# Moving a small transposition, four scalings and the first loads in a two-layer float32 trunk on one Trainium2 core

## The chip, the cores and the metric

The kernel runs on one core of one Trainium2 chip. The metric is device time in microseconds (us): the median of three runs of the kernel before is 1584.31 us (1582.89 to 1584.82).

## The reference, cut to what matters

Two layers over x (256 tokens x 2048 columns), 16 heads of 128. Each layer normalizes x, scales and shifts it by a modulation of the condition c, runs attention, gates it with silu(z), projects it and adds it to x, multiplied by the modulation's third part, the gate.

```python
cond = jax.nn.silu(c)
for i in range(2):
    mod = cond @ mod_w[i] + mod_b[i]
    shift, scale, gate = jnp.split(mod[:, None, :], 3, axis=-1)
    h = rms_norm(x, norm_w[i]) * (1.0 + scale) + shift
    y = mixer(h, w_in[i]) @ w_out[i]   # layer 0: 3 dilated groups, w_in 2048 x 20480
    x = x + gate * y                   # layer 1: block attention, w_in 2048 x 8192
return rms_norm(x, final_norm_w)
```

## The kernel before, in words

Every weight matrix is read once, in units of two halves (128 rows x 512 columns each, 512 KB a unit). A unit's raw float32 lands in a ring of five buffers; ScalarE rounds it to a high part `wh` (L347) and VectorE subtracts to get the low part `wl` (L353). TensorE multiplies in three products: high by high, high by low, low by high. So VectorE and ScalarE convert while TensorE multiplies, and a ring of four converted units limits how far ahead they can be (`plan_conversions`).

The order is written out by hand. A list of steps is built first; the last loop then emits, for each step `i`: its matmuls, the tasks hung on it with `at_once` (evacuations of PSUM), the low parts of the units whose conversion was emitted one step earlier (`finish_converts`), the new conversions, and the tasks hung on it with `at`. Every engine runs its own instructions in that order. A task at step `i` therefore stands, on each engine's queue, behind all that was emitted up to it.

The modulation of layer 0 and 1 is not a matmul. `mod_unit` loads 512 KB of mod_w and VectorE multiplies it by the broadcast condition and sums it (L143, two instructions of 512 columns); four such units make one 128-wide row of shift and scale.

The places that the change touches:

- **Start.** SyncE loads the small weights, both halves of x (`xin`, 128 tokens each), four mod units, then weights. `start_rstd` (L199) sums squares, on VectorE for the first half of x and on ScalarE for the second. GpSimd scales x (L234), TensorE transposes it.
- **First 256 steps.** Each is one half unit by one 128-row chunk k of the normalized input ("row k"). Row k exists only after four of its mod units: `rows_ready(k)` (L248) adds them up and writes `hA` high (L256) and low (L262). `READY` (L579) says at which step each row may be used first; the mod units of row k are hung on the steps before, and `rows_ready(k)` on `READY[k] - 3`. A planner (L584) then lays out visits: it takes the output part that is least far along and multiplies all rows that are ready. The first visit of a part ends in a copy on ScalarE (L565), each later one in two additions on VectorE (L567).
- **Gate.** Mod units of the third part are spread over later steps by `add_pieces` (L171). At the step after the last one `gate_write` (L155) sums them on VectorE (L149), transposes the 128 x 16 result on TensorE into `pgt` (L161), copies it and writes it to DRAM; `gate_read` broadcasts it back. This happens once per layer. The gate is used in the output projection, hundreds of steps later in both layers.
- **Border.** Between the layers `norm_transpose` (L723) transposes x with the scale on the diagonal (L728) and applies scale and shift to four blocks of 128 columns, n of them on VectorE (L736) and the others on ScalarE (L738); `norm_split` makes the high part on ScalarE (L194) and the low part on VectorE (L195). Step `mid` ends the first half of the tokens, `last` the second.

Of the kernel before, what the change touches and what calls it, by code (L numbers as in the profile page):

```python
# [12 lines left out]
F32 = mybir.dt.float32  # L13
F32R = mybir.dt.float32r
AF = mybir.ActivationFunctionType
ALU = mybir.AluOpType
AX = mybir.AxisListType

P = 128
S = 256  # L20
D = 2048
# [3 lines left out]
EPS = 1e-6  # L25
# [28 lines left out]
def trunk_kernel(ctx: ExitStack, tc: tile.TileContext, x, c, small_w, mod_t, weights, final_norm_w, dmask, out, laid_out):  # L54


    nc = tc.nc
    pool = lambda name, bufs, **k: ctx.enter_context(tc.tile_pool(name=name, bufs=bufs, **k))
    const = pool("const", 1)
# [6 lines left out]
    tmpp = pool("tmpp", 1)  # L66
    small = pool("small", 4)
    actp = pool("actp", 1)
# [9 lines left out]
    x_v = x[0].rearrange("(m a) d -> m a d", a=2)  # L78
# [5 lines left out]
    xin = [ypool.tile([P, D], F32, name=f"xin{i}", tag=f"y{2 + i}") for i in range(2)]  # L84
# [1 line left out]
    for i in range(2):  # L86
        nc.scalar.dma_start(c_row[i][0:1], c[:, i * 1024:(i + 1) * 1024])
    smalls = const.tile([P, 128], F32, name="smalls")
    nc.sync.dma_start(smalls, small_w)
    nwT, mbT = smalls[:, 0:2 * KC], smalls[:, 2 * KC:]  # L90
    gate = [const.tile([P, 1024], F32, name=f"gate{i}") for i in range(2)]
    dm = const.tile([P, 9 * P], F32, name="dm")
# [4 lines left out]
    nhalf = const.tile([P, 2], F32, name="nhalf")  # L97
    nc.gpsimd.memset(nhalf, -0.5)
    cb = [const.tile([P, 512], F32, name=f"cb{i}") for i in range(4)]
    eps = const.tile([P, 1], F32, name="eps")  # L100
    nc.gpsimd.memset(eps, EPS)
    modq = const.tile([P, 96, 4], F32, name="modq")
    modc = const.tile([P, 96], F32, name="modc")
    sc0 = const.tile([P, KC], F32, name="sc0")
# [30 lines left out]
    def mod_unit(layer, b, half):  # L135

        early = layer == 0 and b < 32 and b % 16 > 0
        raw = next(early_raw) if early else rawp.tile([P, 1024], F32, name="raw", tag="raw")
        nc.sync.dma_start(raw, mod_t[layer, b, half])
        m = 48 * layer + b  # L140
        for i in range(2):
            part, q = raw[:, i * 512:(i + 1) * 512], 2 * half + i
            nc.vector.tensor_tensor_reduce(part, part, cb[q], 1.0, 0.0 if q else mbT[:, m:m + 1],  # L143
                                           ALU.mult, ALU.add, modq[:, m, q:q + 1])

    def mod_sums(m, n, step=1):

        cols = slice(m, m + (n - 1) * step + 1, step)
        nc.vector.tensor_reduce(modc[:, cols], modq[:, cols], axis=AX.X, op=ALU.add)  # L149
# [5 lines left out]

    def gate_write(layer):

        mod_sums(48 * layer + 32, 16)
        scratch[layer] = dram.tile([KC, P], F32, name=f"gate_rows{layer}", tag=f"g{layer}")
        pt = ps_y.tile([P, 512], F32, name="pgt", tag="y")  # L160
        nc.tensor.transpose(pt[:KC, :P], modc[:, 48 * layer + 32:48 * layer + 48], ident)  # L161
        rows = small.tile([P, P], F32, name="grows", bufs=1)
        nc.scalar.activation(rows[:KC], pt[:KC, :P], AF.Copy)
        nc.gpsimd.dma_start(scratch[layer], rows[:KC])
# [6 lines left out]
    def add_pieces(i0, i1, layer, part):  # L171

        for n in range(32):
            at(i0 + n * (i1 - i0) // 32, mod_unit, layer, 16 * part + n // 2, n % 2)
        if part == 2:
            at(i1 + 1, gate_write, layer)
            at(i1 + 3, gate_read, layer)

    def scale_b():
        mod_sums(48, 32)  # L180
# [3 lines left out]
    def rstd_of(ss, n):  # L184

        r = small.tile([P, 2], F32, name="rstd")
        nc.vector.tensor_scalar(r[:, :n], ss, 1.0 / D, EPS, op0=ALU.mult, op1=ALU.add)
        nc.gpsimd.tensor_tensor(r[:, :n], r[:, :n], nhalf[:, :n], op=ALU.pow)
        return r

    def split(dst, src):

        hi = dst[:, :, 0]
        nc.scalar.activation(hi, src, AF.Copy)  # L194
        nc.vector.tensor_tensor(dst[:, :, 1], src, hi.bitcast(F32), op=ALU.subtract)  # L195
# [3 lines left out]
    def start_rstd(tt):  # L199
        ss = small.tile([P, 2], F32, name="ss0")  # L200
        sq = tmpp.tile([P, 1024], F32, name="sq", tag="tmp")
        st = small.tile([P, 1], F32, name="ss1")
        if tt == 0:
            for i in range(2):
                xi = xin[tt][:, i * 1024:(i + 1) * 1024]
                nc.vector.tensor_tensor_reduce(sq, xi, xi, 1.0, 0.0, ALU.mult, ALU.add, ss[:, i:i + 1])
            nc.vector.tensor_tensor(st, ss[:, 0:1], ss[:, 1:2], op=ALU.add)
            start_r.append(rstd_of(st, 1))
            return
        for i in range(2):  # L210
            nc.scalar.activation(sq, xin[tt][:, i * 1024:(i + 1) * 1024], AF.Square, accum_out=ss[:, i:i + 1])
            nc.scalar.activation(st, ss[:, i:i + 1], AF.Identity, scale=1.0 / D, bias=st if i else eps)
        r = small.tile([P, 2], F32, name="rstd")
        nc.gpsimd.tensor_tensor(r[:, 0:1], st, nhalf[:, 0:1], op=ALU.pow)
        start_r.append(r)

    def start_first(tt):

        xc = xin[tt][:, 0:P]
        nc.scalar.activation(xc, xc, AF.Copy, scale=start_r[tt][:, 0:1])  # L220
        if tt == 0:
            slots["first"] = ps_s.tile([P, 512], F32, name="pxt", tag="s")
        pt = slots["first"]
        nc.tensor.transpose(pt[:, tt * P:(tt + 1) * P], xc, ident)
        if tt == 1:
            nc.scalar.activation(xnT[0][:, 0], pt[:, 0:S], AF.Copy)
# [101 lines left out]
    def at(i, f, *a):  # L328
        tasks.setdefault(i, []).append((f, a))
# [21 lines left out]
    def finish_converts(c=slice(0, 2)):  # L351
        for raw, wh, wl in to_finish:
            nc.vector.tensor_tensor(wl[:, c], raw[:, c], wh[:, c].bitcast(F32), op=ALU.subtract)  # L353
        if c.stop == 2:
            to_finish.clear()
# [166 lines left out]
    def product(p, key, st, n, u, first, last):  # L522
        def pe():
            moving(group_ps(key), st, (2 * u, 2 * u + 1), conv[n], (0, 1), first, last)
        return add_step(n, pe)
# [51 lines left out]

    first_parts = [(0, p) for p in PARTS] + [(1, p) for p in PARTS[:EARLY]]
    READY = [0]  # L579
    for n in (9, 9, 10, 11, 11) + (12,) * 10:  # L580
        READY.append(READY[-1] + n)
    done = [0] * len(first_parts)
    visits, t = [], 0
    while min(done) < KC:  # L584
        n_ready = sum(r <= t for r in READY)
        n = done.index(min(done)) if n_ready < KC else next(i for i, d in enumerate(done) if d < KC)
# [18 lines left out]
    for k in range(1, KC):  # L605
        i0, i1 = READY[k - 1], READY[k]
# [8 lines left out]
    for j in range(1, 4):  # L615
# [4 lines left out]
        for n, p in enumerate(PARTS[EARLY:] if j == 1 else PARTS):  # L620
# [3 lines left out]
            for u in range(8):  # L624
                m = add_unit(wA, u, COL[p] * D + j * GC)
                i = product(p, ("A", j, p), st_a, m, u, u == 0, u == 7)
# [79 lines left out]
    b0, mid, last = out_steps("A", "a_w_out", epilogue("A"), True)  # L706
# [7 lines left out]
    hB_box = []  # L714
# [8 lines left out]
    def norm_transpose(tt, g):  # L723
        if not hB_box:
            hB_box.append(hpool.tile([P, KC, 2, S], F32R, name="hB", tag="h"))
        pt = (ps_s, ps_o, ps_t, ps_y)[g].tile([P, 512], F32, name="pxt", tag="soty"[g])
        for b in range(4):
            nc.tensor.matmul(pt[:, b * P:(b + 1) * P], X[g][:, tt, b * P:(b + 1) * P], rB[tt], start=True, stop=True)  # L728
        hf = tp.tile([P, 4, P], F32, name="t")
        hs = tmpp.tile([P, 2, P], F32, name="hs", tag="tmp")  # L730
        n = 3 - g % 2
        for b in range(4):
            k = 4 * g + b
            src, a, s = pt[:, b * P:(b + 1) * P], abB[:, k:k + 1], modc[:, 48 + k:49 + k]
            if b < n:
                nc.vector.tensor_scalar(hf[:, b], src, a, s, op0=ALU.mult, op1=ALU.add)  # L736
            else:
                nc.scalar.activation(hs[:, b - n], src, AF.Identity, scale=a, bias=s)  # L738
        hfB[tt, g] = (n, hf[:, :n], hs[:, :4 - n])

    def norm_split(tt, g):
        n, hf, hs = hfB[tt, g]
        split(hB_box[0][:, 4 * g:4 * g + n, :, tt * P:(tt + 1) * P], hf)
        split(hB_box[0][:, 4 * g + n:4 * g + 4, :, tt * P:(tt + 1) * P], hs)

    for tt, i in enumerate((mid, last)):
        at_once(i, norm_b, tt)
        for g, n in enumerate((3, 5, 9, 11) if tt == 0 else (4, 5, 6, 8)):
            at_once(i + n, norm_transpose, tt, g)
            at(i + n, norm_split, tt, g)  # L750
# [3 lines left out]
    for j in range(4):  # L754
# [4 lines left out]
        for p in PARTS_B:  # L759
            col = COL_B[p] * D + j * GC  # L760
            if j == 0 and p == "v":
                ns = [add_unit(wB, u, col, HOLD[u] if u < 4 else None)
                      for u in range(8)]
                for tt in range(2):
                    for u, n in enumerate(ns):
                        def pe(n=n, u=u, tt=tt, key=("B", j, p)):
                            moving(group_ps(key), st_b, (2 * u, 2 * u + 1), conv[n], (tt,), u == 0, u == 7)
                        i = add_step(n, pe)
            elif p != "v":
                i = whole_part("B", j, p, st_b, wB, col)  # L770
                continue
            else:
                for u in range(8):
                    i = product(p, ("B", j, p), st_b, add_unit(wB, u, col), u, u == 0, u == 7)
# [4 lines left out]
    b0, mid, last = out_steps("B", "b_w_out", epilogue("B"), False)  # L779
# [30 lines left out]


    plan = plan_conversions()
    for tt in range(2):
        nc.sync.dma_start(xin[tt], x_v[:, tt])
    start_rstd(0)
    start_first(0)
    warm(2)
    for l in range(2):
        m1 = mbT[:, 48 * l + 16:48 * l + 32]
        nc.vector.tensor_scalar(m1, m1, 1.0, None, op0=ALU.add)  # L820
    for n in range(4):
        mod_unit(0, 16 if n < 2 else 0, n % 2)
    start_rstd(1)
    start_first(1)
    warm(1)
    for g in range(4):
# [9 lines left out]
    for i, (n, pe) in enumerate(steps):  # L836
        pe()
        for f, a in first_tasks.get(i, []):
            f(*a)
        finish_converts()  # L840
        for m in plan.get(i, []):
            convert(m)
        for f, a in tasks.get(i, []):
            f(*a)
# [38 lines left out]
```

## Time and profile before

| what | value |
| --- | --- |
| median of three runs | 1584.31 us |
| the profiled execution | 1584.17 us, of which span 1582.1 us |
| TensorE matmul / VectorE / ScalarE busy | 98% / 71% / 48% of the span |
| mean granted TensorE clock | 0.994 of full speed |
| DMA | 380.77 MB, mean 241 GB/s |

A share near 100% on TensorE says that it sets the pace and that time can be won only where it waits or runs at the lower clock. What ends its waits is in the view of waits; where they lie is in the order of time of each engine.

### The profile page before, as it was taken

What the parts mean: (1) busy time and instruction counts of PE and PEld (TensorE: products, weight loads), DVE (VectorE), ACT (ScalarE), POOL (GpSimd) and SP (SyncE); (2) the same over time, 40 slices, a digit from 0 to 9 for tenths busy, and PEclk for the clock granted to TensorE, in tenths of its full rate; (3) what the DMA queues carried; (4) which work ended last, traced back from release to release, by engine and by line L of the source; (5) the groups of instructions that cost most, each with busy time, mean ns of one, the idle gap of its engine ahead of it and who ended that gap; (6) DMA issues with size and microseconds to landing.
All of it is one profiled execution on the core that took longest, in us unless ns stands there. A gap on an engine that the chain in (4) does not pass through costs nothing. (4 is left out here: it accounts for less than half of the span.)

```text
span 1582.1 us, 23691 instructions
## 1 busy us (share of the span) xinstructions
PE 1555.3 (98%) x8960; PEld 1366.4 (86%) x8960; DVE 1128.3 (71%) x2008; ACT 757.4 (48%) x1041; POOL 30.3 (2%) x35
## 2 busy tenths in 40 slices
PE   8999999999999998999999999999999998999997
PEld 6898899999988887888888888888888887888886
DVE  7889887667678766777777775766448887465666
ACT  7644444445444544444544444554545455455542
POOL 4000000000000000000000000000000000000000
PEclk9999999999999999999999999999999999999999
DMA  9978997553788577888578886364467896645543
GB/s 347 344 284 312 317 314 266 189 170 128 236 301 281 187 237 269 303 289 294 205 242 285 294 303 225 129 239 147 135 211 245 295 325 226 213 173 200 187 172 108
DMA packets 104726, 380.77 MB, mean 241 GB/s; under 512 B 11650, under 2 KB 11810, under 8 KB 104356
## 3 DMA queue, kind: packets, MB, share of 16 engines
q1 hardware_dynamic: 102528, 372.95, 67.8%
q0 software_dynamic: 1504, 5.26, 1.0%
q8 instruction: 70, 1.15, 0.3%
q10 hardware_dynamic: 580, 1.06, 0.2%
q14 instruction: 44, 0.36, 0.1%
HBM read 377.10 MB, written 2.11 MB: 240 GB/s over the span
## 5 line engine op out<-in xcount | busy, mean ns | idle before, releaser
L347 ACT ACTIVATE wh<-raw 128x1024 fp32r<-128x1024 f32 (+1 forms) x505 | 527.3, 1056 | 519.1 <-PE acc L297 174.1
L353 DVE TENSOR_TENSOR wl<-raw,wh 128x1024 fp32r<-128x1024 f32 (+1 forms) x505 | 609.0, 1221 | 192.3 <-ACT wh L347 190.8
L297 PE MATMUL acc<-hA,wh 128*128 128x512 f32 x1152 | 289.4, 393 | 0.0
L297 PEld LDWEIGHTS acc<-hA,wh 128*128 128x128 f32 x1152 | 207.8, 189 | 36.7
L297 PE MATMUL acc<-hB,wh 128*128 128x512 f32 x768 | 197.2, 396 | 0.0
L284 PE MATMUL acc<-hA,wh 128*128 128x256 f32 x640 | 182.8, 286 | 1.0 <-ACT hA L256 1.0
L285 PE MATMUL acc<-hA,wh 128*128 128x256 f32 x640 | 182.0, 284 | 0.6 <-DVE hA L262 0.6
L286 PE MATMUL acc<-hA,wl 128*128 128x256 f32 x640 | 181.8, 284 | 0.0
L302 PEld LDWEIGHTS acc<-hA,wl 128*128 128x128 f32 x1152 | 157.8, 191 | 11.8
L302 PE MATMUL acc<-hA,wl 128*128 128x256 f32 x1152 | 161.1, 283 | 0.0
L297 PEld LDWEIGHTS acc<-hB,wh 128*128 128x128 f32 x768 | 138.0, 189 | 23.9
L273 PE MATMUL acc<-wh,hA 128*128 128x512 f32 x384 | 156.0, 406 | 1.0 <-DVE hA L258 1.0
L275 PE MATMUL acc<-wh,hA 128*128 128x512 f32 x384 | 151.1, 394 | 0.4 <-DVE hA L262 0.4
L274 PE MATMUL acc<-wl,hA 128*128 128x512 f32 x384 | 150.6, 392 | 0.0
L143 DVE CUSTOM_DVE_ANT_0 raw<-raw,cb 128x512 f32<-128x512 f32 x198 | 131.1, 689 | 18.4 <-DMA raw<-in_mod_t_dram 18.4
L284 PEld LDWEIGHTS acc<-hA,wh 128*128 128x128 f32 x640 | 123.5, 193 | 1.4 <-ACT hA L256 1.2
L285 PEld LDWEIGHTS acc<-hA,wh 128*128 128x128 f32 x640 | 123.6, 193 | 1.0 <-DVE hA L262 0.8
L286 PEld LDWEIGHTS acc<-hA,wl 128*128 128x128 f32 x640 | 123.5, 193 | 0.0
L302 PEld LDWEIGHTS acc<-hB,wl 128*128 128x128 f32 x768 | 106.0, 191 | 8.6 <-DVE wl L353 0.4
L302 PE MATMUL acc<-hB,wl 128*128 128x256 f32 x768 | 109.0, 284 | 0.2 <-DVE wl L353 0.2
L275 PEld LDWEIGHTS acc<-wh,hA 128*128 128x128 f32 x384 | 72.4, 189 | 17.1 <-DVE hA L262 1.3
L273 PEld LDWEIGHTS acc<-wh,hA 128*128 128x128 f32 x384 | 72.7, 189 | 15.9 <-ACT hf L259 2.2
(235 smaller groups left out, 1780.7 us busy)
## 6 DMA issues: line engine op xcount, KB each, us to landing
raw<-in_weights_dram SPq DMA_DIRECT2D x512, 512.0 KB, 4.4
raw<-in_mod_t_dram SPq DMA_DIRECT2D x132, 512.0 KB, 4.7
gate<-in_mod_t_dram SPq DMA_DIRECT2D x40, 512.0 KB, 5.3
dm<-in_mod_t_dram SPq DMA_DIRECT2D x20, 512.0 KB, 5.3
xin<-in_x_dram SPq DMA_DIRECT2D x2, 1024.0 KB, 6.2
gate<-gate_rows POOLq DMA_DIRECT2D x4, 512.0 KB, 6.9
x<-in_x_dram POOLq DMA_DIRECT2D x4, 512.0 KB, 6.4
fw<-in_final_norm_w_dram POOLq DMA_DIRECT2D x2, 512.0 KB, 4.7
```

What stands on the lines that cost most here:

```text
L143: nc.vector.tensor_tensor_reduce(part, part, cb[q], 1.0, 0.0 if q else mbT[:, m:m + 1], ALU.mult, ALU.add, modq[:, m, q:q + 1])
L273: nc.tensor.matmul(o, hi, wh[:, i], start=f, stop=False, skip_group_check=True)
L274: nc.tensor.matmul(o, hi, wl[:, i], start=False, stop=False, skip_group_check=True)
L275: nc.tensor.matmul(o, lo, wh[:, i], start=False, stop=l, skip_group_check=True)
L284: nc.tensor.matmul(o, wh[:, i, wc], hi, start=first and h % 2 == 0, stop=False, skip_group_check=True)
L285: nc.tensor.matmul(o, wh[:, i, wc], lo, start=False, stop=False, skip_group_check=True)
L286: nc.tensor.matmul(o, wl[:, i, wc], hi, start=False, stop=last, skip_group_check=True)
L297: nc.tensor.matmul(ps_of(h), ws[u][0][:, i, cols(h)], both, start=us[u] == 0 and i == 0, stop=low_first and us[u] == 7 and i == 1, skip_gr ...
L302: nc.tensor.matmul(ps_of(h)[:, 0:S], ws[u][1][:, i, cols(h)], st(2 * us[u] + i)[:, 0, :], start=False, stop=not low_first and us[u] == 7 a ...
L347: nc.scalar.activation(wh[:, c], raw[:, c], AF.Copy)
L353: nc.vector.tensor_tensor(wl[:, c], raw[:, c], wh[:, c].bitcast(F32), op=ALU.subtract)
```

## The change

The gate's sums stay at the step after the last unit, but its transposition and write go seven steps later and the read seven too. Of the second half of x, VectorE squares the first 1024 columns and ScalarE the other 1024; the variable `eps` falls away, since the sum starts at EPS. The first loads go x's first half, small weights, two mod units, x's second half, two mod units. `READY` is spaced wider at the start and closer at the end. At the border, for the first half of the tokens and the first two column groups, all four blocks are scaled on VectorE; and at the two steps before `last` the low parts are not made, but after the work hung on `last`.

```diff
 def gate_write(layer):
-    mod_sums(48 * layer + 32, 16)
     ...
     if part == 2:
-        at(i1 + 1, gate_write, layer)
-        at(i1 + 3, gate_read, layer)
+        at(i1 + 1, mod_sums, 48 * layer + 32, 16)
+        at(i1 + 8, gate_write, layer)
+        at(i1 + 10, gate_read, layer)
 def start_rstd(tt):
     ...
-    for i in range(2):
-        nc.scalar.activation(sq, xin[tt][:, i * 1024:(i + 1) * 1024], AF.Square, accum_out=ss[:, i:i + 1])
-        nc.scalar.activation(st, ss[:, i:i + 1], AF.Identity, scale=1.0 / D, bias=st if i else eps)
+    sq2 = actp.tile([P, 1024], F32, name="sq2", tag="a7")
+    nc.vector.tensor_tensor_reduce(sq, xin[tt][:, 0:1024], xin[tt][:, 0:1024], 1.0 / D, EPS, ALU.mult, ALU.add,
+                                   ss[:, 0:1])
+    nc.scalar.activation(sq2, xin[tt][:, 1024:D], AF.Square, accum_out=ss[:, 1:2])
+    nc.scalar.activation(st, ss[:, 1:2], AF.Identity, scale=1.0 / D, bias=ss[:, 0:1])
-for n in (9, 9, 10, 11, 11) + (12,) * 10:
+for n in (10, 10, 11, 11, 11) + (12,) * 6 + (11,) * 4:
     READY.append(READY[-1] + n)
 def norm_transpose(tt, g):
-    hs = tmpp.tile([P, 2, P], F32, name="hs", tag="tmp")
-    n = 3 - g % 2
+    n = 4 if tt == 0 and g < 2 else 3 - g % 2
+    hs = tmpp.tile([P, 2, P], F32, name="hs", tag="tmp") if n < 4 else hf
 def norm_split(tt, g):
-    split(hB_box[0][:, 4 * g + n:4 * g + 4, :, tt * P:(tt + 1) * P], hs)
+    if n < 4:
+        split(hB_box[0][:, 4 * g + n:4 * g + 4, :, tt * P:(tt + 1) * P], hs)
+late_low = range(last - 2, last)
-for tt in range(2):
-    nc.sync.dma_start(xin[tt], x_v[:, tt])
+nc.sync.dma_start(xin[0], x_v[:, 0])
+nc.sync.dma_start(smalls, small_w)
 start_rstd(0)
 ...
-for n in range(4):
-    mod_unit(0, 16 if n < 2 else 0, n % 2)
+mod_unit(0, 16, 0)
+mod_unit(0, 0, 0)
+nc.sync.dma_start(xin[1], x_v[:, 1])
 start_rstd(1)
+mod_unit(0, 16, 1)
+mod_unit(0, 0, 1)
     ...
-    finish_converts()
+    if i not in late_low:
+        finish_converts()
```

## Rows read from the trace of the kernel before

**Rows 1.** The page, busy us and share of each engine: TensorE.
```profile
PE 1555.3 (98%) x8960; PEld 1366.4 (86%) x8960; DVE 1128.3 (71%) x2008; ACT 757.4 (48%) x1041; POOL 30.3 (2%) x35
```

**Rows 2.** Waits of TensorE: us in total, times, longest us.
```profile
PE pgt L161 <- DVE modc L149: 9.0, 2, 4.8
...
PE acc L273 <- ACT hB L194: 1.2, 1, 1.2
...
PE acc L284 <- ACT hA L256: 1.0, 1, 1.0
...
PE acc L285 <- DVE hA L262: 0.6, 1, 0.6
PE acc L275 <- DVE hA L262: 0.4, 2, 0.2
```

**Rows 3.** TensorE in order of time, 600 to 614: start, us, what [idle].
```profile
609.57 0.28 PE L161 MATMUL pgt<-ident,modc 128*16 128x128 f32 x1 [4.80 <-DVE modc L149]
```

**Rows 4.** VectorE in order of time, 590 to 618.
```profile
605.74 2.36 DVE L353 TENSOR_TENSOR wl<-raw,wh 128x1024 fp32r<-128x1024 f32 x2 [2.89 <-ACT wh L347]
...
609.30 0.22 DVE L149 TENSOR_REDUCE modc<-modq 128x16 f32<-128x64 f32 x1
```

**Rows 5.** Windows: length, busy PE, PEld, DVE, ACT, POOL, granted clock, DMA.
```profile
610.00:613.00 3.00, 3.00 (x10) 2.51 (x9) 0.73 (x4) 0.15 (x1) 0.71 (x1) 0.50 0.76 231
1340.50:1343.50 3.00, 3.00 (x12) 2.61 (x11) 0.07 (x1) 1.35 (x2) 0.08 (x1) 0.50 0.44 168
98.10:101.10 3.00, 3.00 (x16) 3.00 (x15) 2.95 (x6) 0.73 (x1) 0.00 (x0) 0.50 0.78 229
```

**Rows 6.** TensorE in order of time, 256 columns a matmul, twelve a step.
```profile
92.80 0.28 PE L284 MATMUL acc<-hA,wh 128*128 128x256 f32 x1
92.92 0.28 PE L285 MATMUL acc<-hA,wh 128*128 128x256 f32 x1
```

**Rows 7.** TensorE in order of time, 512 columns a matmul, six a step.
```profile
1065.75 0.39 PE L273 MATMUL acc<-held,yA 128*128 128x512 f32 x1
1065.98 0.39 PE L274 MATMUL acc<-held,yA 128*128 128x512 f32 x1
```

**Rows 8.** VectorE in order of time, 60 to 104: modulation, low part, evacuation, row.
```profile
64.28 0.75 DVE L143 CUSTOM_DVE_ANT_0 gate<-gate,cb,smalls 128x512 f32<-128x512 f32 x1
...
64.95 0.69 DVE L143 CUSTOM_DVE_ANT_0 gate<-gate,cb 128x512 f32<-128x512 f32 x1
...
65.56 1.22 DVE L353 TENSOR_TENSOR wl<-raw,wh 128x1024 fp32r<-128x1024 f32 x1
...
69.79 1.28 DVE L567 TENSOR_TENSOR actA0v<-actA0v,acc 128x512 f32<-128x512 f32 x2
...
94.36 0.16 DVE L149 TENSOR_REDUCE modc<-modq 128x2 f32<-128x8 f32 x1
...
95.87 0.43 DVE L262 TENSOR_TENSOR hA<-hf,hA 128x256 fp32r<-128x256 f32 x1 [1.16 <-ACT hf L259]
```

**Rows 9.** ScalarE in order of time, the same row's high part.
```profile
94.75 0.60 ACT L256 ACTIVATE hA<-xnT,modc,sc 128x256 fp32r<-128x256 f32 x1 [2.25 <-DVE sc L252]
```

**Rows 10.** VectorE in order of time, the start.
```profile
6.37 1.23 DVE L206 CUSTOM_DVE_ANT_0 sq<-xin 128x1024 f32<-128x1024 f32 x1 [6.37 <-DMA xin<-in_x_dram]
...
10.31 0.75 DVE L143 CUSTOM_DVE_ANT_0 raw<-raw,cb,smalls 128x512 f32<-128x512 f32 x1 [0.89 <-ACT cb L112]
...
14.72 0.98 DVE L143 CUSTOM_DVE_ANT_0 raw<-raw,cb 128x512 f32<-128x512 f32 x1
...
15.74 0.16 DVE L149 TENSOR_REDUCE modc<-modq 128x2 f32<-128x8 f32 x1
```

**Rows 11.** DMA issued at 2.1 to 2.3: count, KB, us to landing.
```profile
raw<-in_mod_t_dram SPq DMA_DIRECT2D x1, 512.0 KB, 8.0
```

**Rows 12.** GpSimd in order of time, the start.
```profile
13.98 17.70 POOL L234 TENSOR_SCALAR xin<-xin,rstd 128x384 f32<-128x384 f32 x8
```

**Rows 13.** VectorE in order of time, the border.
```profile
1081.81 1.05 DVE L736 TENSOR_SCALAR t<-pxt,abB,modc 128x128 f32<-128x128 f32 x3 [0.64 <-PE pxt L728]
```

More of the change, by code (lines that the diff above doesn't have):

```diff
@@ L88, in trunk_kernel @@
     smalls = const.tile([P, 128], F32, name="smalls")
-    nc.sync.dma_start(smalls, small_w)
     nwT, mbT = smalls[:, 0:2 * KC], smalls[:, 2 * KC:]
@@ L99, in trunk_kernel @@
     cb = [const.tile([P, 512], F32, name=f"cb{i}") for i in range(4)]
-    eps = const.tile([P, 1], F32, name="eps")
-    nc.gpsimd.memset(eps, EPS)
     modq = const.tile([P, 96, 4], F32, name="modq")
```

## The prediction

> **What bounds the kernel now.** First the busy times: TensorE's matmuls cover 98% of the span, VectorE 71%, ScalarE 48% [rows 1]. Of a kernel like this the reader should expect one thing only: time goes or comes where TensorE stands still or runs slowly. So the second view is TensorE's waits [rows 2]. By far the largest is `pgt` waiting for `modc`, 9.0 us in two pieces; behind it come the rows of the first stage (`hA`: 1.0, 0.6 and 0.4 us) and the border (`hB`: 1.2 us). The third view is the order of time around the big one [rows 3]: the transposition waited 4.80 us and then took 0.28. VectorE's order of time says why [rows 4]: it was itself idle for 2.89 us until ScalarE had the high parts, then made two low parts (2.36 us), and only after them came the small sum at 609.30, which TensorE needs. None of that is needed by the matmuls behind the transposition; they stand still because they are queued behind it. The fourth view is the granted clock by windows [rows 5]: right after each of the two stalls, and right after the row waits at 95 to 97 us, it is 0.50 (1.2 GHz instead of 2.4).
>
> **What a stretch at the lower clock costs.** Each of the three windows [rows 5] is 3.0 us with TensorE busy throughout at half speed, a loss of at least 1.5 us; such a stretch looks a little longer than the window, so I take 1.7 us each. That is my estimate from these rows.
>
> **The gate.** The sums stay where they are; the transposition goes seven steps on. A step of the later stages is at least the twelve-matmul or six-matmul kind: 12 x 0.12 = 1.44 us or 6 x 0.23 = 1.36 us [rows 6, 7], so seven steps are about 9.7 us of TensorE work, against sums that came 4.80 us too late [rows 3]. Both waits go: -9.0 us [rows 2]. With them goes what follows on them, two stretches at the lower clock: 2 x -1.7 = -3.4 us. What is late next? The two low parts that held up the sums belong to units that TensorE reaches only several steps later, and VectorE had nothing queued when they came [rows 4], so I expect no new wait there. Nothing but the write and read of the gate on GpSimd's queue waits for the transposition, and its reader comes hundreds of steps later. Sum of this part: -12.4 us.
>
> **The rows spaced wider.** This looks like pure relief: row 5 is now used first at step 53 instead of 50. But `READY` also decides the visits. I ran the planner's rule by hand on both lists. Before it gives 55 visits, now 59; with 16 first visits each way, VectorE's evacuations go from 39 to 43, and they begin earlier. Before, the first one stands at step 31. Now the visits of steps 25-26, 27-28, 29-31, 32-34, 35-37, 38-40, 41-44 and 45-48 all end in one. VectorE's prices: a mod unit (two instructions) 0.67 + 0.61 = 1.28 us by their starts, an evacuation 1.28, from the row's sums to its low part 95.87 + 0.43 - 94.36 = 1.94, to its high part 94.75 + 0.60 - 94.36 = 0.99 [rows 8, 9]; a low part 2.36 / 2 = 1.18 [rows 4].
>
> Row 3 (first used at step 31, made at step 28, both by the listing). Call the end of step 28 T; TensorE wants the row two steps later, T + 2.72 [rows 7]. From the end of step 26 at T - 2.72 VectorE has an evacuation, a low part and a mod unit, 3.74 us, so it is at T + 1.02; then the evacuation and the low part of step 28, T + 3.48; the high part of the row at T + 4.47, 1.75 late, the low one at T + 5.42, where the third product wants it at 4.47 + 0.46: another 0.5. Row 3 is 2.2 us late. Before, it was made at step 25, without evacuation or low part at that step, and is not among the waits.
>
> Row 5 (used at 53, made at 50). From the end of step 34 to its making VectorE has 5 evacuations, 9 low parts, 6 mod units and row 4: 6.4 + 10.6 + 7.7 + 1.9 = 26.6 us; TensorE's 16 steps take 23.0 [rows 6]. So T + 3.6, the high part at T + 4.6 against 2.88: 1.7 late, and 0.8 more for the low one. If the stretch at the lower clock after row 3 lets VectorE catch up, some of that goes: I take 2.0. Row 7 (used at 77): 5 evacuations, 11 low parts, 7 mod units and row 6, 30.3 us, against 21 steps, 29.1; between on time and 1.2 late, I take 0.6.
>
> Together 4.8 us of waiting, and as the 1.6 us at row 5 brought the lower clock before [rows 2, 5], I count one stretch each after rows 3 and 5: 4.8 + 3.4 = 8.2 us. What falls away is 1.0 + 0.6 + 0.4 + 1.7 = 3.7. Net +4.5 us. Bounds: if no row is late, -3.7; if all three are late in full with three stretches, 2.2 + 2.5 + 1.2 + 5.1 - 3.7 = +7.3. I take the counted value, because the same count puts row 5 of before late and row 3 in time.
>
> **The start.** VectorE is the chain: it was free at 9.42 and waited 0.89 us [rows 10]. The profile names ScalarE's `cb`, but the first condition block is long done; the first mod unit, issued from 2.12, landed after 8.0 us [rows 11], at 10.1. With 1 MB of x moved behind two mod units, those land before VectorE is free: up to 0.9 us gained. Against it the squares of half of x's second half, 1.23 us [rows 10], now stand between the mod units on VectorE; ScalarE's shorter sum was not on this chain. The last two units wait for nothing, since the bytes ahead of them are the same. 0.9 gained, 1.3 lost, and perhaps 0.4 from x going ahead of the small weights: I take 0. Bounds -0.9 and +1.3.
>
> The Trainium skill, "SBUF — State Buffer", section "SBUF: two separate sides", says that GpSimd and a VectorE instruction with two SBUF inputs hold a shared port exclusively, the other blocking for the whole instruction. GpSimd's eight scalings take 17.70 us from 13.98 on [rows 12], 2.2 each; the mod instruction that begins under them took 0.98 instead of 0.69 [rows 8, 10], 0.3 more and not 2.2. The later mod units put about one more instruction under them: +0.3 by the row, +2.2 by the rule; the sum uses neither.
>
> **The border.** Three scalings of 0.35 us (1.05 / 3) [rows 13] come onto VectorE, at most +1.1 us; ScalarE's leave the chain, and two low parts now stand behind x's last addition instead of ahead of it. But the scaling that ends TensorE's 1.2 us wait [rows 2] is still queued behind those low parts. Bounds -1.2 (the whole wait) and +1.1. I take -0.3, near nothing.
>
> **Sum.** -12.4 + 4.5 + 0 - 0.3 = -8.2 us. The profiled execution took 1584.17 us, as good as the median 1584.31, so 1576.0 us.
>
> **The rivals.** *No row is later than before* (0.25): the wider spacing outweighs the evacuations. For it: row 5 gets three steps more; against it the count above. Between 1571.5 (rows as before) and 1567.8 (all their waits gone); 1570.
>
> *Rows late to the end of the stage* (0.05), the one that ends slower. With 12 steps a row, VectorE has 5.1 of mod units, 7.1 of low parts, 1.9 of row and two evacuations, 2.6: 16.7 us against 17.3 of TensorE [rows 4, 6, 8], 0.6 to spare, too little to work off a lag at once; with the last rows at 11 steps there is none. Each further late row costs about 2.0 + 1.7 = 3.7; from the third one on (rows 9, 11, 14) the gain is gone: 1576.0 + 11.1 = 1587.1. Against it: no late row after 5 before.
>
> *The gate's stall stays* (0.04): the change doesn't do what it says, because the sums are still behind something at seven steps. 1576.0 + 12.4 = 1588.4. Only a VectorE lag of over 9 us would do it, and none shows.
>
> *GpSimd blocks VectorE at the start* (0.04), the rule above as a mechanism: one mod instruction more held up for one scaling, 2.2 us, before the first product: 1578.2. That instruction's 0.3 [rows 8, 10] speaks against it.
>
> **How the numbers follow.** The forecast has 0.62. Its own bounds (rows -3.7 to +7.3, border, start) are wide; I let the range run from 1569 to 1580, which leaves out the deep end of the first rival and the two slow ones, under 0.2. Below 1581.1 counts as faster by over 0.2% (3.2 us, about what a measurement of this kernel can tell from no change): forecast, first and last rival, 0.91; about half of the second falls within, 0.03; the rest and the third, slower, 0.06.
>
> **What would show it.** Right: `pgt` gone from TensorE's waits, the clock 1.00 there; new waits on `hA` at steps 31 and 53 (about 62 to 70 and 97 to 105 us), each of 1.5 to 2.5 us, VectorE without idle time before them, the lower clock behind them; 43 evacuations of two on L567. Wrong: no wait on `hA` at all (first rival), more than three of them (second), `pgt` still there (third), a first product more than 1.5 us from its old place.

## The result, and the profile after

The changed kernel takes 1575.07 us (median of 4 runs, 1573.21 to 1576.23), the kernel before 1584.31 beside it (4 runs, 1582.89 to 1584.82): a ratio of 0.9942, with an interval of 0.9925 to 0.9959. The forecast was 1576.0 in a range from 1569 to 1580. The profiled execution took 1573.91 us, its span is 1571.8 us, 10.3 less than before.

The page's busy times after; TensorE's share can hardly rise from the 98% of [rows 1]:

```profile
PE 1551.7 (99%) x8960; PEld 1362.7 (87%) x8960; DVE 1135.3 (72%) x2019; ACT 754.1 (48%) x1033; POOL 31.3 (2%) x34
```

TensorE's waits after (us in total, times, longest), which answer to [rows 2]:

```profile
PE acc L283 <- ACT hA L255: 1.8, 1, 1.8
PE acc L301 <- DVE wl L352: 1.2, 1, 1.2
PE acc L284 <- DVE hA L261: 1.1, 2, 0.6
...
PE acc L272 <- ACT hA L255: 0.9, 1, 0.9
PE acc L272 <- DVE hA L257: 0.7, 1, 0.7
PE acc L274 <- DVE hA L261: 0.5, 2, 0.3
PE acc L272 <- ACT hB L191: 0.4, 1, 0.4
```

The 9.0 us on `pgt` are gone. In their place stand rows that come late (`hA`) and one wait that was not forecast, on `wl`. (Line numbers are a few lower than before.) Where each lies, TensorE's order of time shows (start, us, what, idle time ahead of it and what ended it):

```profile
66.13 0.50 PE L272 MATMUL acc<-wh,hA 128*128 128x512 f32 x1 [0.93 <-ACT hA L255]
...
67.08 0.50 PE L274 MATMUL acc<-wh,hA 128*128 128x512 f32 x1 [0.21 <-DVE hA L261]
...
100.29 0.38 PE L283 MATMUL acc<-hA,wh 128*128 128x256 f32 x1 [1.79 <-ACT hA L255]
...
101.24 0.40 PE L284 MATMUL acc<-hA,wh 128*128 128x256 f32 x1 [0.57 <-DVE hA L261]
...
621.24 0.27 PE L157 MATMUL pgt<-ident,modc 128*16 128x128 f32 x1
...
638.10 1.22 PE L301 MATMUL acc<-hA,wl 128*128 128x256 f32 x8 [1.21 <-DVE wl L352]
```

The windows that answer to [rows 5] (length, busy PE, PEld, DVE, ACT, POOL, granted clock, DMA share, GB/s), and one around the new wait:

```profile
610.00:613.00 3.00, 3.00 (x15) 2.48 (x14) 2.98 (x8) 0.90 (x1) 0.00 (x0) 1.00 0.95 310
...
102.00:105.00 3.00, 3.00 (x17) 3.00 (x16) 3.00 (x7) 1.06 (x1) 0.00 (x0) 0.52 0.84 291
...
634.00:638.00 4.00, 2.89 (x17) 2.37 (x15) 2.47 (x6) 0.09 (x1) 0.00 (x0) 1.00 0.82 334
```

At 610 the clock is 1.00 where it was 0.50; after row 5's wait it is 0.52. At 634 to 638 TensorE lacks 1.1 us of 4.

A total hides terms of opposite sign. What opens it up is the start of the same matmul in both traces, taken at several places. The table gives its start less that in the kernel before, in us:

| TensorE reaches | changed | gate alone | changed, again | write later | all, old spacing |
|---|---|---|---|---|---|
| first product (17 us) | -0.3 | | -0.2 | | |
| step 256 (407 us) | +1.1 | -1.6 | +2.2 | +1.3 | -4.3 |
| behind the first gate's old place (631 us) | -5.2 | -7.9 | -3.9 | -5.2 | -10.4 |
| behind the new wait (about 650 us) | -3.7 | -6.3 | -1.8 | -5.2 | -10.4 |
| behind the border (1118 us) | -4.5 | -6.3 | -2.6 | -5.9 | -11.1 |
| before the second gate (1305 us) | -4.9 | -6.7 | -3.0 | | |
| behind the second gate | -10.4 | -12.2 | -8.4 | | |
| end | -10.3 | -12.2 | -8.4 | -11.7 | -16.9 |

The columns are named after the kernels of the experiments below. In the changed kernel the first stage costs, the first gate gives 6.3 and hands 1.5 back, and the second gives 5.5.

### The profile page after: what moved, and what is told of

It is laid out like the page before. It is cut to its first block, busy times and chain, and to the rows that moved or that the text cites. A ratio compares the mean times of both kernels' runs of the same rounds, so it can differ in the third digit from the quotient of the medians.

```text
span 1571.8 us, 23691 instructions
## 1 busy us (share of the span) xinstructions
PE 1551.7 (99%) x8960; PEld 1362.7 (87%) x8960; DVE 1135.3 (72%) x2019; ACT 754.1 (48%) x1033; POOL 31.3 (2%) x34
## 4 chain that ended last, share of the span: by engine, by line
PE 89%; DVE 1%; DMA 0%; ACT 0%; issue 0%; POOLq 0%; POOL 0%; DVEq 0%; ACTq 0%
PE acc L296 28%; PE acc L301 14%; PE acc L274 10%; PE acc L272 10%; PE acc L273 10%; PE acc L284 3%; PE acc L285 3%; PE acc L283 3%; PE po L460 2%; PE pss L442 2%; PE pst L423 1%; PE po L493 1%; PE pss L477 1%; DMA raw<-in_mod_t_dram 0%; DVE wl L352 0%; PE pxt L727 0%
```

## The experiments

They ran in three groups, each on one chip together with the kernel before, which took 1585.05 us beside the first four, 1584.29 beside the next four and 1583.46 beside the last two. Ratios and intervals are against it.

**The gate's edit alone**, on the kernel before:

```diff
 def gate_write(layer):
-    mod_sums(48 * layer + 32, 16)
...
-    at(i1 + 1, gate_write, layer)
-    at(i1 + 3, gate_read, layer)
+    at(i1 + 1, mod_sums, 48 * layer + 32, 16)
+    at(i1 + 8, gate_write, layer)
+    at(i1 + 10, gate_read, layer)
```

> The kernel before with the gate's part alone: sums at the old step, transposition and write seven steps later, read seven later. Theory: both waits of the transposition go (9.0 us) and the two stretches at 1.2 GHz behind them (3.4 us), and the read of the gate, now among the weights' transfers without the stall's reserve, gives back 1.2 to 1.5 us in the first layer: 1584.3 - 11.0 = about 1573.3 us, row waits as before at step 50. Rival (the new wait for a low part at 638 us is chance and has nothing to do with the read): 1571.9 us, no wait on L302 between 620 and 660 us.

Measured: 1573.57 us (1571.98 to 1574.73), ratio 0.9928 [0.9914, 0.9941]. That is as much as the whole change gives, or a little more: the rest of the change, taken together, gives nothing, and beside the changed kernel on the same chip (1575.91, below) it costs some 2 us. Two rows of its trace, TensorE's order of time and the window behind row 5's wait:

```profile
635.54 1.21 PE L302 MATMUL acc<-hA,wl 128*128 128x256 f32 x8 [1.35 <-DVE wl L353]
```

```profile
97.00:103.00 6.00, 6.00 (x53) 6.00 (x52) 6.00 (x12) 1.93 (x2) 0.00 (x0) 1.00 0.76 277
```

The new wait on `wl` comes with the gate's edit, not with the other edits. And the lower clock that followed row 5's wait before is missing here, with the same old spacing: the 1.6 us at step 256 in the table are that one stretch.

**The changed kernel with the old spacing:**

```diff
-for n in (10, 10, 11, 11, 11) + (12,) * 6 + (11,) * 4:
+for n in (9, 9, 10, 11, 11) + (12,) * 10:
```

> The changed kernel with the old spacing (9, 9, 10, 11, 11, then 12 each). Theory (the wider list costs 3.3 us net, by its earlier visits' additions on VectorE): waits on hA at step 50 alone, about 1.6 us, and a stretch at 1.2 GHz perhaps; step 256 reached 3 us earlier than with the new spacing; 1575.1 - 3 = about 1572 us. Rival (the start is earlier, so the first rows need the wider spacing): waits of over 1 us at steps 9 and 18 and more than 2 us at 50, time 1575 to 1578 us.

Measured: 1573.07 us (1572.1 to 1574.1), ratio 0.9925 [0.9912, 0.9937]. The waits from 20 to 140 us are the old ones again:

```profile
PE acc L283 <- ACT hA L255: 1.0, 1, 1.0
PE acc L284 <- DVE hA L261: 0.6, 1, 0.6
...
PE acc L274 <- DVE hA L261: 0.2, 1, 0.2
```

**The changed kernel again**, unedited, on the same chip:

> The changed kernel once more, beside the other three. Theory: waits on hA at steps 31, 53 and 77 of about 1.7, 2.6 and 1.2 us as in its first profile, and 1.2 us at 638 us, since they come from the order of work; 1575 us. What is open: whether a stretch at 1.2 GHz at 19 us, which the first profile did not have and the kernel before had, comes back; with it the time is 1.7 us more. Rival (the waits are chance of one execution): they lie elsewhere.

Measured: 1575.91 us (1574.64 to 1576.76), ratio 0.9943 [0.993, 0.9955], with the same waits at the same places; the one on `wl` is 1.9 us here. Unlike the first profile of this kernel, this one has a stretch at the lower clock at 18 us, as the kernel before has. Against the old spacing that is 2.8 us more, and the two sets of runs don't overlap: the wider spacing costs, as forecast, but less than the forecast 4.5.

**The gate's read twenty steps later**, to see whether it brings the wait on `wl`:

```diff
-    at(i1 + 10, gate_read, layer)
+    at(i1 + 30, gate_read, layer)
```

> The changed kernel with the gate's read twenty steps later again (30 instead of 10 after the last unit). Theory (the 1 MB read beside the weights' transfers makes the wait of 1.2 us at 638 us): that wait goes from its place; 1574 us, and it may come back where the read now lies if the reserve there is as thin. Rival (chance, or the lost reserve alone): the wait at 638 us stays, 1575 us.

Measured: 1575.48 us (1574.75 to 1575.77), ratio 0.994 [0.9926, 0.9953]. The wait stayed. But the edit didn't move the read, as GpSimd's and TensorE's order of time show, one row of each:

```profile
627.26 1.09 POOL L165 DMA_DIRECT2D gate<-gate_rows  x2 [4.42 <-DVE actA2q L547]
```

```profile
638.68 1.21 PE L301 MATMUL acc<-hA,wl 128*128 128x256 f32 x8 [1.93 <-DVE wl L352]
```

GpSimd had nothing else in its queue, so a read that stands twenty steps later in the program was issued at 627.26, in the changed kernel at 627.86. Nothing follows on the cause from this run.

**The write itself later** for the first gate, so that the read has to wait for it:

```diff
-    at(i1 + 8, gate_write, layer)
-    at(i1 + 10, gate_read, layer)
+    at(i1 + (8 if layer else 62), gate_write, layer)
+    at(i1 + (10 if layer else 64), gate_read, layer)
```

> The changed kernel with the first layer's transposition, write and read 54 steps later again. In the run with the read alone later, GpSimd issued it at 627 us all the same, since nothing else stands on its queue; here the transposition holds it. Theory (the 1 MB read beside the weights' transfers makes the wait at 638 us): that wait, 1.2 to 1.9 us in four profiles, goes from its place, 1574.3 us, unless it comes back at the new place. Rival (the reserve that the old stall gave is lacking there, read or no read): the wait stays at 636 to 640 us, 1575.9 us.

Measured: 1572.96 us (1572.58 to 1573.62), ratio 0.9931 [0.9917, 0.9945]. The first fence is of this kernel: the read's issue on GpSimd; then its window at the old place of the wait.

```profile
725.99 1.09 POOL L165 DMA_DIRECT2D gate<-gate_rows  x2 [5.32 <-DVE wl L352]
```

```profile
634.00:638.00 4.00, 4.00 (x27) 3.65 (x26) 4.00 (x7) 2.12 (x2) 0.00 (x0) 1.00 0.75 248
```

TensorE is busy throughout, and no new wait comes up behind the read's new place. The DMAs issued between 626 and 634 us (count, KB each, median us to landing) tell why, first in the changed kernel, then in this one:

```profile
raw<-in_weights_dram SPq DMA_DIRECT2D x3, 512.0 KB, 8.3
...
gate<-gate_rows POOLq DMA_DIRECT2D x2, 512.0 KB, 8.2
```

```profile
raw<-in_weights_dram SPq DMA_DIRECT2D x3, 512.0 KB, 5.2
```

With the gate's 1 MB on the way at the same time the weights land 3 us later. VectorE's order of time shows what that does in the changed kernel: VectorE stands idle for its next modulation unit, which holds up the low parts behind it, and TensorE wants these. With the later write (last row) the idle time is 2.0 us shorter:

```profile
635.53 0.75 DVE L140 CUSTOM_DVE_ANT_0 raw<-raw,cb,smalls 128x512 f32<-128x512 f32 x1 [4.83 <-DMA raw<-in_mod_t_dram]
...
636.82 3.49 DVE L352 TENSOR_TENSOR wl<-raw,wh 128x1024 fp32r<-128x1024 f32 x3
```

```profile
633.51 0.75 DVE L140 CUSTOM_DVE_ANT_0 raw<-raw,cb,smalls 128x512 f32<-128x512 f32 x1 [2.81 <-DMA raw<-in_mod_t_dram]
```

So the read, moved behind the transposition, meets transfers that TensorE soon needs. By the table this wait costs 1.5 us in the first execution of the changed kernel (-5.2 to -3.7) and 2.1 in the second. All seven profiles with the read at 623 to 629 us have it, of 0.9 to 2.1 us; the three with the later write have none there.

Slower transfers alone are not enough, though. The second gate's read, moved by the same seven steps to 1350 us, brings no wait. And at its new place the first one slows the weights as well, as the DMAs issued from 724 to 734 us in the kernel with the later write show, while TensorE waits for nothing:

```profile
raw<-in_weights_dram SPq DMA_DIRECT2D x4, 512.0 KB, 7.2
```

**Ten additions left out.** The forecast put the late rows down to four more visits, begun earlier. This kernel leaves out the additions of the ten visits that end before step 60 and so doesn't compute the whole result:

```diff
-at_once(i, evac_visit, ("visit", v), j, p, k0 == 0)
+if k0 == 0 or i >= 60:
+    at_once(i, evac_visit, ("visit", v), j, p, k0 == 0)
```

> The changed kernel without VectorE's additions of the ten visits that end before step 60 (two instructions, 1.28 us each time); their partial sums are left out of the result. Theory (these additions stand ahead of the rows on VectorE's queue): no wait on hA of over 0.3 us at steps 31 and 53, and no stretch at 1.2 GHz after 53; step 256 about 6 us earlier, 1575.9 - 6 = about 1570 us. Rival (the rows wait for their modulation transfers): the waits stay at 1.7 and 2.6 us.

Measured: 1568.85 us in one run. Step 256 comes 6.1 us earlier than in the changed kernel's second profile. The waits from 60 to 140 us, all that is left of them:

```profile
PE acc L284 <- DVE hA L261: 0.6, 1, 0.6
```

The waits of rows 3 and 5 are gone, row 7's 0.6 stays. So VectorE's additions make those two rows late, and not the rows' own transfers. The run takes away all ten early additions, not only those that the wider spacing added.

**The rows' own work two steps earlier**, the rival remedy, nothing left out:

```diff
-at(max(0, i1 - 4 - (3 - n) * (i1 - i0) // 4), mod_unit, 0, (16 if n < 2 else 0) + k, n % 2)
-at(i1 - 3, rows_ready, k)
+at(max(0, i1 - 6 - (3 - n) * (i1 - i0) // 4), mod_unit, 0, (16 if n < 2 else 0) + k, n % 2)
+at(i1 - 5, rows_ready, k)
```

> The changed kernel with each row of the first stage made two steps earlier, its mod units too (READY - 5 in place of READY - 3, the units' 4 replaced by 6). Theory (the rows are late on VectorE's queue by 1.7 to 2.6 us, and two steps are 2.8 us): the waits on hA at steps 31, 53 and 77 go or fall below 0.5 us, and the stretch at 1.2 GHz after 53 with them; 1575.9 - 6 = about 1570 us. Rival (the modulation's transfers are what is late): the waits stay, 1575 to 1576 us.

Measured: 1572.57 us (1571.95 to 1575.08), ratio 0.993 [0.9917, 0.9943]. Row 3 is in time, row 5 is late by 0.4 and 0.6 and row 7 by 0.3, but a new wait came up at row 1. One row of TensorE and one of ScalarE in this kernel:

```profile
34.21 0.39 PE L283 MATMUL acc<-hA,wh 128*128 128x256 f32 x1 [1.67 <-ACT actA0q L564]
```

```profile
32.10 0.60 ACT L255 ACTIVATE hA<-xnT,modc,sc 128x256 fp32r<-128x256 f32 x1 [1.39 <-DVE sc L251]
```

Row 1's high part now stands ahead of evacuations in ScalarE's queue, where it waits 1.39 us for VectorE, and TensorE waits for those evacuations. Row 1 therefore keeps its place in the last two kernels.

**The start's edits alone**, on the kernel before:

```diff
-for tt in range(2):
-    nc.sync.dma_start(xin[tt], x_v[:, tt])
+nc.sync.dma_start(xin[0], x_v[:, 0])
+nc.sync.dma_start(smalls, small_w)
...
-for n in range(4):
-    mod_unit(0, 16 if n < 2 else 0, n % 2)
+mod_unit(0, 16, 0)
+mod_unit(0, 0, 0)
+nc.sync.dma_start(xin[1], x_v[:, 1])
 start_rstd(1)
+mod_unit(0, 16, 1)
+mod_unit(0, 0, 1)
```

> The kernel before with the start's part alone (order of the first loads, VectorE's share of the squares). Theory: VectorE gains at the first mod unit what it spends on the squares, first product 0.3 us earlier, all else as before: 1584.7 us against 1585.05. Rival (the start gains 2 us, as the first profile of the changed kernel had no stretch at 1.2 GHz at 19 us): 1583 us, without that stretch.

Measured: 1584.38 us in 10 runs (1582.59 to 1586.2), ratio 1.000 [0.9991, 1.001]: nothing. The waits for the gate are there, and at them this execution shows the lower clock for longer than [rows 5], in windows with the same columns:

```profile
607.50:613.50 6.00, 5.57 (x19) 4.80 (x20) 1.99 (x8) 1.96 (x3) 0.71 (x1) 0.50 0.86 291
1337.60:1343.60 6.00, 5.54 (x19) 4.77 (x20) 0.78 (x3) 1.93 (x3) 0.63 (x2) 0.50 0.57 178
```

The starts of the same matmuls say that this costs about 1 us more at each gate than in the kernel before. On the other side no stretch follows row 5's wait here, and there is none at 18 us either. The second is worth nothing with the old spacing: TensorE comes sooner to row 1, which is then late, by 0.68 and 0.57 us:

```profile
34.04 0.39 PE L283 MATMUL acc<-hA,wh 128*128 128x256 f32 x1 [0.68 <-ACT hA L255]
```

**Both causes taken away**, in the changed kernel: the write later as above, and the rows from row 2 on two steps earlier; once with the old spacing and once with the new:

```diff
-at(max(0, i1 - 4 - (3 - n) * (i1 - i0) // 4), mod_unit, 0, (16 if n < 2 else 0) + k, n % 2)
-at(i1 - 3, rows_ready, k)
+at(max(0, i1 - (6 if k > 1 else 4) - (3 - n) * (i1 - i0) // 4), mod_unit, 0, (16 if n < 2 else 0) + k, n % 2)
+at(i1 - (5 if k > 1 else 3), rows_ready, k)
```

> What the runs point to, together: the changed kernel with the old spacing, rows from the third on made two steps earlier (the second row of the stage, made for step 9, stays, since its earlier place cost a wait of 1.7 us for PSUM before), and the first layer's gate write 54 steps later. Theory (each removed wait counts by itself): no wait on hA of over 0.5 us after step 9, none at 638 us; step 256 about 2 us earlier than before the change, the gate's stalls and the border as in the changed kernel: about 1569.5 us. Rival (what is removed comes back as another wait): 1572 to 1573 us, like the single steps.

> The same with the new spacing. Theory (the additions only hurt where a row stands behind them, so with earlier rows little is left of the spacing's cost): row 5 about 1.4 us late as in the run with all rows earlier, with or without a stretch at 1.2 GHz; 1.5 us above the same with the old spacing, about 1571 us. Rival (the four additional visits cost by themselves): 3 us above it.

Measured: 1567.79 us (1567.34 to 1567.97), ratio 0.9902 [0.9887, 0.9916], with the old spacing; 1567.57 us (1567.18 to 1568.62), ratio 0.9903 [0.9886, 0.9919], with the new. Both beat the kernel before by nearly 16 us and every other kernel that computes the same, and both are faster than expected (1569.5 and 1571). TensorE's waits from 20 to 140 us in order of time, first old, then new spacing:

```profile
33.83 0.38 PE L283 MATMUL acc<-hA,wh 128*128 128x256 f32 x1 [0.53 <-ACT hA L255]
34.78 0.38 PE L284 MATMUL acc<-hA,wh 128*128 128x256 f32 x1 [0.57 <-DVE hA L261]
```

```profile
97.29 0.38 PE L283 MATMUL acc<-hA,wh 128*128 128x256 f32 x1 [0.40 <-ACT hA L255]
98.25 0.39 PE L284 MATMUL acc<-hA,wh 128*128 128x256 f32 x1 [0.57 <-DVE hA L261]
132.21 0.39 PE L284 MATMUL acc<-hA,wh 128*128 128x256 f32 x1 [0.25 <-DVE hA L261]
```

With the rows made earlier the two spacings take the same time, but they wait at different rows: the old spacing 1.1 us at row 1, the new one 1.2 us at rows 5 and 7. So the four more visits cost only where they make a row late, and the wider spacing of row 1 does save its wait. Neither profile has a stretch at the lower clock at 18 us or behind these waits.

## Why the prediction came out, step by step

The time was right to 0.9 us, but two terms were off by some 2 us each, in opposite directions, so that it came so close is in good part luck. With the terms as measured the sum would be 1584.2 - 10.2 + 2.4 - 0.2 - 0.7 = 1575.5; the changed kernel took 1575.1 and, again, 1575.9 us. The execution with the first profile (1573.9) is faster than that by 1.1 us at step 256 (+1.1 against +2.2 in the second), where it lacks the stretch at the lower clock at 18 us, and by 0.4 at 1250 us, which the kernel before lost there and nearly all others did not.

**The gate: -10.2 (gate alone, first and second gate net: 4.7 + 5.5; in the changed kernel again 4.0 + 5.4) instead of -12.4.** The waits and the lower clock behind them went as forecast: 6.3 us at the first gate, where 4.8 + 1.7 = 6.5 was counted, and 5.5 at the second against 4.2 + 1.7 = 5.9. The step that failed is "I expect no new wait there"; the wait on `wl` came, of 1.2 us in the first profile and 1.9 in the second. The argument looked at VectorE's queue and at who reads the gate; it named the read on GpSimd's queue and did not ask which transfers those two DMAs of 512 KB would now meet. The later write shows that they are the cause (5.2 us to landing instead of 8.3, no wait). Why the old place, seven steps earlier, did no such harm was not tested. The read slowed transfers there too (two modulation loads issued beside it in the kernel before took 7.0 us), but TensorE had no need to wait for them; perhaps because TensorE, standing still there, gave VectorE time to get ahead.

**The rows: about +2.4 instead of +4.5.** That is the way from -0.2 to +2.2 in the second profile, which has the stretch at the lower clock at 18 us as the kernel before has; the medians of the changed kernel and the old spacing say 2.8. VectorE's additions are 86, so 43 evacuations, as counted. The places are the three that were counted: steps 31, 53 and 77. VectorE's order of time in the changed kernel, ahead of row 3's use at 66.13, is the counted queue word for word:

```profile
59.12 1.37 DVE L566 TENSOR_TENSOR actA0v<-actA0v,acc 128x512 f32<-128x512 f32 x2
60.40 1.22 DVE L352 TENSOR_TENSOR wl<-raw,wh 128x1024 fp32r<-128x1024 f32 x1
61.54 0.68 DVE L140 CUSTOM_DVE_ANT_0 dm<-dm,cb 128x512 f32<-128x512 f32 x1
...
62.15 0.69 DVE L140 CUSTOM_DVE_ANT_0 dm<-dm,cb 128x512 f32<-128x512 f32 x1
...
62.76 1.28 DVE L566 TENSOR_TENSOR actA0v<-actA0v,acc 128x512 f32<-128x512 f32 x2
63.96 1.22 DVE L352 TENSOR_TENSOR wl<-raw,wh 128x1024 fp32r<-128x1024 f32 x1
65.10 0.15 DVE L146 TENSOR_REDUCE modc<-modq 128x2 f32<-128x8 f32 x1
65.28 0.16 DVE L251 TENSOR_TENSOR sc<-modc,smalls 128x1 f32<-128x1 f32 x1
```

An addition, a low part, a unit, an addition, a low part, and only then the row's sums, with no idle time between them. Row 3 was 1.1 us late (0.93 + 0.21) against 2.2: VectorE was a microsecond further on than the count had it. Row 5 was 2.4 us late. The count gave 2.5, and was then cut to 2.0 for a stretch at the lower clock after row 3 in which VectorE would catch up; that stretch didn't come, and the plain count was the better number. Row 7 has 0.57 against 0.6. The mis-sized terms are row 3's wait and one of the two stretches, 1.1 + 1.7 = 2.8 of the 8.2; row 5's own 0.4 goes the other way. And of the 3.7 that was to fall away 0.2 stayed: one of the two waits that make up the 0.4 us on L262 [rows 2] is at the first product, which no spacing moves. With these the count gives 5.8 - 3.5 = +2.3.

**The start: 0, as taken**, for -0.3 at the first product and a ratio of 1.000 alone. VectorE's start after answers to [rows 10]:

```profile
8.87 0.75 DVE L140 CUSTOM_DVE_ANT_0 raw<-raw,cb,smalls 128x512 f32<-128x512 f32 x1
...
11.45 1.22 DVE L208 CUSTOM_DVE_ANT_0 sq<-xin 128x1024 f32<-128x1024 f32 x1
...
14.43 0.98 DVE L140 CUSTOM_DVE_ANT_0 raw<-raw,cb 128x512 f32<-128x512 f32 x1
15.45 0.16 DVE L146 TENSOR_REDUCE modc<-modq 128x2 f32<-128x8 f32 x1
```

The first unit begins 1.4 us sooner, the squares of 1.22 go in between, and the sums end 0.3 sooner: gain and loss as counted. The unit under GpSimd's scalings takes 0.98 again, so the rival by which GpSimd blocks VectorE for a whole scaling falls here too: the rule of the Trainium skill ("SBUF — State Buffer", section "SBUF: two separate sides") did not show its 2.2 us in either trace.

**The border: -0.7 instead of -0.3**, by the starts on either side of it (-3.8 to -4.5). The 1.2 us on `hB` became 0.4. VectorE's order of time there:

```profile
1085.70 0.69 DVE L683 TENSOR_TENSOR tmp<-acc,gate 128x512 f32<-128x512 f32 x1 [0.47 <-PE acc L274]
...
1088.78 3.49 DVE L352 TENSOR_TENSOR wl<-raw,wh 128x1024 fp32r<-128x1024 f32 x3
...
1092.19 1.04 DVE L735 TENSOR_SCALAR t<-pxt,abB,modc 128x128 f32<-128x128 f32 x3
```

The scaling is queued behind the low parts, as said, but the additions now come ahead of them, and with the 3.8 us of shift taken off it begins 0.7 us sooner than before (1096.73). The border alone was not run, but all nine profiles with its edits gain 0.7 us there, and the two without them (gate alone, start alone) nothing. Which of its two edits does it stays open.

**The rivals.** *No row is later* falls by the waits at 66 and 100 us. *Rows late to the end of the stage* falls: after step 77 TensorE waits for no further row of this stage. *The gate's stall stays* falls by 621.24, which waits for nothing.

What stays open besides: 0.9 us that the kernel with the old spacing loses between 1236 and 1305 us, and when the lower clock comes (below).

## What to carry to other kernels

An instruction on the bounding engine that needs another engine's late result belongs some steps behind that result; but whatever it issues moves along, so ask of each DMA behind it which transfers it will meet and how soon the bounding engine needs them. To see whether a deadline holds, add up the queue of the engine that serves it from one deadline to the next, at the trace's own durations, and don't soften the count with a clock that may not fall. A wider deadline also moves the work that a planner hangs on it: row 5 gained three steps and came later, and only making the rows earlier as well took most of the waits away.

## What the runs showed of the hardware

**The lower clock is not the same in each execution.** In the twelve profiles here a stretch at 0.50 stands at 18 to 20 us in six, with the old start and with the new one. After row 5's 1.6 us of waiting at step 50 it came in two of four profiles (before and old spacing; not in gate alone and start alone), after the 2.4 us at step 53 in four of four, after the 1.1 us at step 31 in none of four, and after the wait on `wl`, up to 2.1 us long, in none of seven. Behind the gate's 4.8 us TensorE worked some 3.4 us at it in one execution and 5.6 in another. The price of 1.7 us fits the stretch behind row 5 (1.6 us by the table); whether one comes behind a wait this short differs from one execution to the next.

**A later place in the program did not delay a DMA on GpSimd's queue**, which had nothing else in it. Twenty steps later in the program it was issued 0.6 us earlier (627.26 against 627.86); only a dependency held it back (725.99).

**1 MB on GpSimd's queue beside the weights** lengthened three transfers of 512 KB from 5.2 to 8.3 us (medians), at 334 GB/s from 634 to 638 us against 248. At 724 to 734 us, beside the same read, such transfers took 7.2 us, and TensorE waited for none of them.
